# A reordered input stage in a one-core hybrid layer: one meta-token load, its Newton step on ScalarE, table products behind idle ones

## The chip, the cores and the metric

The kernel runs on one core of one Trainium2 chip. The metric is the device time of one launch in microseconds. A core has five engines with a queue of their own each: TensorE (PE, matmuls; PEld is its weight load), VectorE (DVE), ScalarE (ACT), GpSimd (POOL) and SyncE (SP, which here only issues DMAs). ACT issues DMAs too.

## The reference

One decoder layer with two token mixers, on 1024 tokens of width 1024 behind 16 meta tokens, all in float32:

```
h = concat([meta_tokens, x], axis=1)                  # 1040 rows
h = layer_norm(h, in_ln_g, in_ln_b)
z = h @ w_in + b_in                                   # -> q, k, v, conv input, gates
y_attn = sliding_window_attention(q, k, v, sinks, rel_bias) @ w_attn_proj
y_conv = silu(layer_norm(causal_dwconv(val * sigmoid(gate)))) @ w_conv_proj
mixed  = sigmoid(g_attn) * y_attn + sigmoid(g_conv) * y_conv
h = layer_norm(2**0.25 * h + mixed @ w_out, ln1_g, ln1_b)
f = (gelu(g) * u) @ ffn_w_down                        # u, g = causal_dwconv(h @ ffn_w_up)
out = layer_norm(2**0.25 * h + f, ln2_g, ln2_b)[:, 16:]
```

The attention bias depends on the distance of query and key alone, through a table of 32 buckets by 8 heads (`rel_bias`). The first layer norm, the scaled `h` of the first residual, and the rows of that bias table are what this document is about.

## The kernel before, in words

Every large product is done in three passes of a reduced float type: the operands are split into a high part (`hi`, `RHO`) and a rest (`lo`, `RHC`), and PE adds `hi*lo`, `hi*hi`, `lo*hi`. Each weight tile of 128 columns (512 KB) is loaded by SP into one of two raw buffers (`wr`), cast to its high part on ACT (L304) and subtracted to its rest on DVE (L307), and used for all 1040 rows.

The input stage (up to about 56 us) works on tiles of 128 tokens: the meta tokens as tile -1 (`xm`; two copies of the 16 rows, so that a transpose puts them where both neighbours need them) and x0 to x7. `tokens` groups them into (-1), (0, 1), (2, 3, 4), (5, 6, 7). For each group there are these steps, each a small function:

- `stat` (L431): statistics on DVE, two halves of 512 columns and one aggregate per tile;
- `table` (L461): on ACT the approximate inverse root of the variance, `r`;
- `newton` (L466): on DVE one Newton step on `r`, and `m = -mean * r`; four small instructions per group;
- `norm` (L475): `x * r + m`, in two halves, on DVE or ACT;
- `turns` (L492): PE transposes the tile in blocks `k` of 128 columns into PSUM; `scaled` (L505) applies the layer norm's g and b on ACT;
- `parts`, `high`, `low`: the split into `RHO` and `RHC`;
- `z_first` (L546): products of the first three weight tiles `first` (k, v and the first q tile). For the first group of rows, k and v are multiplied unsplit (`raw`).

The order of work on each engine here is written out by hand: `dv`, `ac` and `pe` chain the instructions of DVE, ACT and PE in the order of the text (L572 to L661), and `after` puts one instruction behind another on the same engine without a semaphore. Everything else is ordered by a planner, which takes a priority (`tc.cur_priority`, set by `rank`) and simulated times; loads of the input stage have hand-given ranks 5 to 25, and SP issues them in that order: meta twice (L197), x0, x1, the columns of small parameters (`coll`, `colr`), the second and the first weight tile, x2, the third weight tile, x3 to x7, the fourth weight tile when its buffer is free, the bias table (`tab`), and g and b of the layer norm (`gb`).

PE begins with 20 products of a constant with itself (`ps_w`, L575), whose results nobody uses. The rows of the bias by distance come from two products of `tab` (`ps_v`, L667), 400 and 164 columns wide, placed by the planner behind the input stage; DVE copies them to `vrow` (L668), SP stores `vrow` to `v1d`, spreads that over 128 rows in DRAM (`vd`), and loads from it the skewed `bias` tiles of attention.

`residual` (L288) forms `alpha * h` for the first residual from `x`, the mean, `r`, and the vectors `gb`, and stores it to `h0d`. On its first call it scales `gb` by alpha (L291), on DVE, behind the fourth weight tile's split (`last_split[3]`). All of it runs on DVE from about 50 to 75 us, while PE works on the next weight tiles. The convolution's 31 taps per channel block (L729) then fill DVE up to attention.

Of the kernel before, what the change touches and what calls it, by code (L numbers as in the profile page):

```python
# [38 lines left out]
NH = 8  # L39
# [9 lines left out]
ALPHA = 2.0 ** 0.25  # L49
# [30 lines left out]
J_BAND, J_META, J_META0, J_METAQ, J_LEN = 0, 384, 400, 544, 564  # L80
# [32 lines left out]
def tile_hybrid_layer(  # L113
# [3 lines left out]
    nc = tc.nc  # L117
# [5 lines left out]
    def load(o, i):  # L123
        return nc.sync.dma_start(out=o, in_=i)
# [57 lines left out]

    eps = const2.tile([P, 1], F, name="eps")
    nsink = const2.tile([P, 2 * NH], F, name="nsink")[:, :NH]
    with rank(0):
        nc.vector.memset(eps, EPS)
        nc.scalar.activation(nsink[:, 0:1], eps, AF.Abs_reciprocal_sqrt)

# [5 lines left out]
        nc.gpsimd.memset(xm[32:64], 0.0)  # L194
        nc.gpsimd.memset(xm[64:96], 0.0)
    with rank(5):
        for i in range(2):  # L197
            load(xm[i * NMETA:(i + 1) * NMETA], meta_tokens)
    xt = []

    def load_x(j):
# [15 lines left out]
    cff, ident = (coll[:, a - n_right:b - n_right] for a, b in COLS[2:-1])  # L217


    tab = sp.tile([P, J_LEN + NH], F, name="tab")  # L220
    with rank(0):
        nc.gpsimd.memset(tab, 0.0)
    with rank(25):
        load(tab[:33], table_in)

    def bcol(m):
        return colA[:, m:m + 1]
# [58 lines left out]
    gb_scaled = []  # L286

    def residual(src, mu, rs, n, first, dst):  # L288
        if not gb_scaled:
            gb_scaled.append(1)  # L290
            after(nc.vector.tensor_scalar(gb, gb, ALPHA, None, OP.mult), last_split[3])  # L291
        src = src[:n]
        nc.vector.scalar_tensor_tensor(src, src, mu[:n], gb[:n, 0], OP.subtract, OP.mult)
        nc.vector.scalar_tensor_tensor(src, src, rs[:n], gb[:n, 1], OP.mult, OP.add)
        load(dst, src[first:n])

# [134 lines left out]
    def stat(t, *js):  # L431

        J = len(tokens[t])
        if t not in norms:
            norms[t] = [sp.tile([P, J, 2], F, name=f"mv{t}")] + [sp.tile([P, J], F, name=f"{n}{t}") for n in "trm"]
        for j in js:
            x_, n = src_of(j)
            st_ = small.tile([P, 2, 6], F, name="st")
            for i in range(2):
                dv(V.bn_stats(st_[:n, i], x_[:, i * 512:(i + 1) * 512]))  # L440
            dv(V.bn_aggr(norms[t][0][:n, tokens[t].index(j)], st_[:n].rearrange("p a b -> p (a b)")))
# [19 lines left out]
    def table(t):  # L461
        mv, t_, r_, m_ = norms[t]
        n = src_of(tokens[t][0])[1]
        ac(nc.scalar.activation(r_[:n], mv[:n, :, 1], AF.Abs_reciprocal_sqrt, bias=eps[:n], scale=1.0))

    def newton(t):  # L466
        n = src_of(tokens[t][0])[1]
        mv, t_, r_, m_ = (x_[:n] for x_ in norms[t])
        stt = V.scalar_tensor_tensor
        dv(stt(t_, mv[:, :, 1], EPS, r_, OP.add, OP.mult))  # L470
        dv(stt(t_, t_, -0.5, r_, OP.mult, OP.mult))
        dv(stt(r_, t_, 1.5, r_, OP.add, OP.mult))
        dv(stt(m_, mv[:, :, 0], -1.0, r_, OP.mult, OP.mult))

    def norm(t, j, on_dve):  # L475
        x_, n = src_of(j)
        i = tokens[t].index(j)
        mv, t_, r_, m_ = norms[t]
        xns[j] = sp.tile([P, D], F, name="xn", tag="xn", bufs=4) if j >= 0 else xm
        to = xns[j] if j >= 0 else xm[96:]  # L480
        for a in range(0, D, 512):
            if on_dve:
                dv(V.tensor_scalar(to[:, a:a + 512], x_[:, a:a + 512], r_[:n, i:i + 1], m_[:n, i:i + 1], OP.mult, OP.add))
            else:
                ac(nc.scalar.activation(to[:, a:a + 512], x_[:, a:a + 512], AF.Identity, bias=m_[:n, i:i + 1],
                                        scale=r_[:n, i:i + 1]))
        later.append((x_, mv[:n, i, 0:1], r_[:n, i:i + 1], n, j))

    GT = [(-1, 0, 1), (2, 3, 4), (5, 6, 7)]
    turned, tms = {}, {}  # L490
# [42 lines left out]
    def whigh(i):  # L533
        ac(nc.scalar.copy(first[i][0], first[i][2]))
# [36 lines left out]

    tc.cur_priority = RK_START  # L572
    warm = pat.tile([P, 512], F, name="ps_w", tag="o")
    for i in range(20):
        pe(nc.tensor.matmul(warm[:, :P], ones, ones, start=True, stop=True))  # L575
# [12 lines left out]
    stat(2, 2)  # L588
    scaled(0, 0)
# [8 lines left out]
    evac(0, 0)  # L598
    stat(2, 3)
    stat(2, 4)  # L600
    whigh(1)
    table(2)
    z_first(0, (1,), *range(8), raw=True)
    evac(0, 1)
    newton(2)
# [54 lines left out]
        evac(2, i)  # L660
    first_nm = dv_done[-1]  # L661

    tc.cur_priority = RK_RESID + 1000
    vrow = sp.tile([P, J_LEN + 104], F, name="vrow")[:NH, :J_LEN]
    for a, b in ((0, 400), (400, J_LEN)):
        ps = pat.tile([P, 512], F, name="ps_v", tag="o" if a == 0 else "t", bufs=1 if a == 0 else 2)
        after(nc.tensor.matmul(ps[:NH, :b - a], tab[:, J_LEN:], tab[:, a:b], start=True, stop=True), pe_done[-1])  # L667
# [5 lines left out]
    tc.cur_priority = RK_RESID  # L673
    for src, mu, rs, n, j in later:
        if j >= 0:
            residual(src, mu, rs, n, 0, h0d[2 + j * P:2 + (j + 1) * P, :])
        else:
            residual(src, mu, rs, NMETA, U0, h0d[0:2, :])
    start.close()
# [1121 lines left out]
def packed(i):  # L1801

    def by_channel(*vs):
        return np.concatenate([np.reshape(v, (-1, P)) for v in vs]).T

    def heads(a):

        n = a.shape[1:]
        return a.reshape((NKV, NH // NKV, HD) + n).swapaxes(0, 1).reshape((CW,) + n)

    def tiles(w, c):

# [39 lines left out]
```

## Time and profile before

| | |
|---|---|
| median of 3 runs | 1262.14 us (1261.92 to 1262.55) |
| the profiled execution | 1261.79 us, span 1260.0 us |
| mean granted TensorE clock | 0.997 |
| PE busy | 1245.9 us (99%) |
| DVE, ACT busy | 1076.2 us (85%), 595.2 us (47%) |
| HBM read, written | 150.29 MB, 62.70 MB |

The span runs from the first to the last instruction of the profiled execution; its time as a launch is 1.8 us longer. Rows of the timeline give the start (us), the time taken (us), engine, line, operation, output and inputs, how many instructions of that form follow each other, and in brackets how long the engine was idle before and what ended that. Rows of the chain of waits give start, share in us, and engine, output and line. A row of the waits by engine gives engine, line, what it waited for, and the total, count and longest of these waits.

### The profile page before, as it was taken

The numbers are of one execution on the slowest core, as the hardware profiler recorded it, in microseconds if no ns is written. First come the engines' busy times: TensorE is split into PE (matmuls) and PEld (weight loads), VectorE is DVE, ScalarE is ACT, GpSimd is POOL, SyncE is SP. The second block draws the span as 40 slices with busy tenths as digits, with TensorE's granted clock in tenths as the row PEclk, the third lists the DMA queues.
The fourth block names the chain that finished last, engine by engine and source line by source line (L and its number), as shares of the span: only waits on it lengthen the run. The fifth ranks groups of instructions, "written<-read, shape, count | busy, mean of one in ns | idle before, by whom it ended". The sixth has DMA issues, their size and how long they took to land.

```text
span 1260.0 us, 23038 instructions
## 1 busy us (share of the span) xinstructions
PE 1245.9 (99%) x9186; PEld 1179.6 (94%) x9186; DVE 1076.2 (85%) x1858; ACT 595.2 (47%) x1100; POOL 7.9 (1%) x9
## 2 busy tenths in 40 slices
PE   8999999999999999999999999999999999999997
PEld 7999999999999999788899999999999998888886
DVE  7888999999978677448999999998989977996697
ACT  7532355655474233344655455455555544545330
POOL 0000000001000000000000000000000000000000
PEclk9999999999999999999999999999999999999999
DMA  6375633433256564221245545454454567998712
GB/s 255 104 253 148 183 108 97 106 93 85 72 155 172 167 166 118 84 99 70 67 161 204 188 171 214 160 209 139 159 205 160 196 227 251 394 357 320 271 63 84
DMA packets 98702, 212.19 MB, mean 168 GB/s; under 512 B 11412, under 2 KB 38612, under 8 KB 98339
## 3 DMA queue, kind: packets, MB, share of 16 engines
q1 hardware_dynamic: 84474, 199.64, 47.6%
q10 hardware_dynamic: 14120, 11.08, 2.8%
q8 instruction: 72, 1.18, 0.4%
q14 instruction: 36, 0.29, 0.1%
HBM read 150.29 MB, written 62.70 MB: 169 GB/s over the span
## 4 chain that ended last, share of the span: by engine, by line
PE 94%; DVE 3%; DMA 1%; ACT 1%; issue 1%; SPq 0%; DVEq 0%; ACTq 0%
PE px L1553 15%; PE py L1553 9%; PE ps_x L1698 9%; PE ps_z L342 8%; PE ps_z L345 8%; PE ps_z L346 8%; PE ps_p L1152 7%; PE ps_z L1698 5%; PE pz L1553 5%; PE pw L1553 5%; PE ps_w L342 2%; PE ps_w L345 2%; PE ps_w L346 2%; PE ps_z L560 2%; PE ps_t L923 1%; PE ps_h L503 1%
## 5 line engine op out<-in xcount | busy, mean ns | idle before, releaser
L342 PE MATMUL ps_z<-RHO,w 128*128 128x256 f32 (+2 forms) x864 | 243.4, 282 | 0.0
L345 PE MATMUL ps_z<-RHO,w 128*128 128x256 f32 (+2 forms) x864 | 242.3, 280 | 0.0
L346 PE MATMUL ps_z<-RHC,w 128*128 128x256 f32 (+2 forms) x864 | 242.2, 280 | 0.0
L342 PEld LDWEIGHTS ps_z<-RHO,w 128*128 128x128 f32 x864 | 162.5, 188 | 1.1 <-ACT FA L709 0.7
L345 PEld LDWEIGHTS ps_z<-RHO,w 128*128 128x128 f32 x864 | 162.5, 188 | 0.5
L346 PEld LDWEIGHTS ps_z<-RHC,w 128*128 128x128 f32 x864 | 162.7, 188 | 0.2
L729 DVE SCALAR_TENSOR_TENSOR FA<-cin,cdw,FA 128x1026 f32<-128x1026 f32 x120 | 154.3, 1296 | 0.7
L1375 DVE TENSOR_TENSOR RHO<-wr,RHO 128x512 fp32r<-128x512 f32 x94 | 63.6, 685 | 8.5 <-ACT RHO L1374 8.5
L304 ACT CAST w<-wr 128x1024 fp32r<-128x1024 f32 x37 | 38.8, 1048 | 61.9 <-PE ps_z L346 47.5
L1374 ACT CAST RHO<-wr 128x512 fp32r<-128x512 f32 x94 | 56.6, 619 | 22.7 <-DVE wr L1392 11.4
L1392 DVE TENSOR_TENSOR wr<-wr 128x512 f32<-128x512 f32 x88 | 60.2, 684 | 0.1
L738 ACT ACTIVATE FA<-ps_z,colr 128x258 f32<-128x258 f32 (+1 forms) x64 | 30.1, 472 | 60.5 <-PE ps_z L346 50.2
L307 DVE TENSOR_TENSOR w<-wr,w 128x1024 fp32r<-128x1024 f32 x37 | 45.1, 1218 | 9.5 <-ACT w L304 9.3
L1565 ACT COPY FA<-px 128x514 f32<-128x514 f32 (+2 forms) x23 | 13.2, 572 | 78.7 <-PE px L1553 78.7
L1152 PE MATMUL ps_p<-OC,w 128*128 128x256 f32 (+1 forms) x384 | 48.1, 278 | 0.0
L1152 PE MATMUL ps_p<-OA,w 128*128 128x256 f32 (+1 forms) x384 | 47.8, 278 | 0.0
L1152 PEld LDWEIGHTS ps_p<-OC,w 128*128 128x128 f32 x384 | 46.2, 188 | 0.1
L1152 PEld LDWEIGHTS ps_p<-OA,w 128*128 128x128 f32 x384 | 45.9, 188 | 0.0
L1375 DVE TENSOR_TENSOR w<-wr,w 128x512 fp32r<-128x512 f32 x60 | 40.6, 686 | 4.7 <-ACT w L1374 4.7
L1553 PE MATMUL px<-OA,RHO 128*128 128x258 f32 x324 | 43.2, 282 | 0.0
L1480 ACT ACTIVATE FA<-OB,coll 128x512 f32<-128x512 f32 x44 | 35.9, 816 | 14.7 <-DVE OB L1561 14.7
L1374 ACT CAST w<-wr 128x512 fp32r<-128x512 f32 x60 | 36.3, 618 | 12.3 <-DVE wr L1392 5.1
(443 smaller groups left out, 3088.1 us busy)
## 6 DMA issues: line engine op xcount, KB each, us to landing
wr<-in_w_up_dram SPq DMA_DIRECT2D x44, 512.0 KB, 3.6
wr<-in_w_z_dram SPq DMA_DIRECT2D x29, 512.0 KB, 4.0
OB<-in_w_down_dram SPq DMA_DIRECT2D x24, 512.0 KB, 4.9
fd<-FA SPq DMA_DIRECT2D x44, 256.0 KB, 2.0
FA<-sd SPq DMA_DIRECT2D x15, 512.0 KB, 8.7
qt<-qd SPq DMA_DIRECT2D x28, 256.0 KB, 5.0
OB<-td SPq DMA_DIRECT2D x14, 512.0 KB, 8.7
sgd<-FA ACTq DMA_DIRECT2D x48, 128.0 KB, 3.3
```

The costliest lines, as they stand in the source:

```text
L304: ins = nc.scalar.copy(hi, raw)
L307: return nc.vector.tensor_tensor(lo, raw, f32(hi), OP.subtract)
L342: ins = nc.tensor.matmul(ps, al, bh, start=i == 0, stop=False)
L345: nc.tensor.matmul(ps, ah, bh, start=False, stop=False)
L346: last = nc.tensor.matmul(ps, ah, bl, start=False, stop=i == n - 1)
L729: nc.vector.scalar_tensor_tensor(acc[c], cin[:, j:j + U], wc, acc[c], OP.mult, OP.add)
L1152: nc.tensor.matmul(ps[:, :b - a], x, rhs(k, hl, a, b), start=k + j == 0, stop=k == 3 and j == 2)
L1374: nc.scalar.copy(hi, src)
L1375: ins = nc.vector.tensor_tensor(lo, src, f32(hi), OP.subtract)
L1392: ins = nc.vector.tensor_tensor(*x)
L1553: ins = nc.tensor.matmul(o, x[:, ks], bmat(sub, q, hl, k), start=first and k + j == 0, stop=k == 3 and j == 2, skip_group_check=not first)
L1698: nc.tensor.matmul(banks[i], l[:, ts], r[:, ws], start=first and a and x + k == 0, stop=z and x == len(ops) - 1 and k == 2, skip_group_che ...
```

## The change

- `meta_tokens` is laid out twice on the host, and one load of 32 rows takes the place of two of 16.
- `tab` is cleared on DVE, not GpSimd, at the head of DVE's queue, and loaded through ACT's DMA queue ahead of ACT's first activation, not late on SP's.
- Idle products: 15, not 20. The two `ps_v` products follow directly behind them. Their PSUM copies: 164 columns on DVE behind `scales`, 400 columns on ACT at the end of its chain. `vrow` is stored from there at a higher rank.
- Meta's Newton step runs on ACT (`newton_act`, seven activations), so that `newton(0)` leaves DVE's chain. The normalization of `xm` stands in two halves on ACT, the second behind `table(1)`.
- `table(2)` stands ahead of the cast of the second weight tile (`whigh(1)`).
- Ranks of the first three weight loads: 13, 16, 19 in place of 14, 13, 16. The order of loads becomes x0, x1, columns, first weight tile, x2, second weight tile, x3, x4, third weight tile, x5 and so on.
- `gb` is scaled at the end of DVE's chain, ahead of the fourth weight tile's rest; the residual's first instruction on each tile except x0 is put behind that rest.

```diff
     with rank(0):
         nc.vector.memset(eps, EPS)
-        nc.scalar.activation(nsink[:, 0:1], eps, AF.Abs_reciprocal_sqrt)
+        nc.vector.memset(tab, 0.0)
+        tab_in = store(tab[:33], table_in)
+        after(nc.scalar.activation(nsink[:, 0:1], eps, AF.Abs_reciprocal_sqrt), tab_in)
...
-        for i in range(2):
-            load(xm[i * NMETA:(i + 1) * NMETA], meta_tokens)
+        load(xm[:2 * NMETA], meta_tokens)
...
-    tab = sp.tile([P, J_LEN + NH], F, name="tab")
-    with rank(0):
-        nc.gpsimd.memset(tab, 0.0)
-    with rank(25):
-        load(tab[:33], table_in)
...
-    def residual(src, mu, rs, n, first, dst):
-        if not gb_scaled:
-            gb_scaled.append(1)
-            after(nc.vector.tensor_scalar(gb, gb, ALPHA, None, OP.mult), last_split[3])
+    def residual(src, mu, rs, n, first, dst, behind=True):
         src = src[:n]
-        nc.vector.scalar_tensor_tensor(src, src, mu[:n], gb[:n, 0], OP.subtract, OP.mult)
+        ins = nc.vector.scalar_tensor_tensor(src, src, mu[:n], gb[:n, 0], OP.subtract, OP.mult)
+        if behind:
+            after(ins, last_split[3])
...
-        with rank({1: 14, 2: 13, 3: 16, 4: 23}.get(n, RK_SPLIT)):
+        with rank({1: 13, 2: 16, 3: 19, 4: 23}.get(n, RK_SPLIT)):
...
+            if n == 4:
+                after(last_split[-1], gb_scale)
...
+    c15 = sp.tile([P, 1], F, name="c15")
+    nc.vector.memset(c15, 1.5)
...
+    def newton_act(t):
+        n = src_of(tokens[t][0])[1]
+        mv, t_, r_, m_ = (x_[:n] for x_ in norms[t])
+        act = lambda *x, **y: ac(nc.scalar.activation(*x, AF.Identity, **y))
+        act(m_, mv[:, :, 0], scale=-1.0)
+        act(t_, mv[:, :, 1], bias=eps[:n], scale=1.0)
+        for i in range(2):
+            act(t_, t_, scale=r_)
+        act(t_, t_, bias=c15[:n], scale=-0.5)
+        act(t_, t_, scale=r_)
+        act(m_, m_, scale=t_)
+        norms[t][1:3] = norms[t][2:0:-1]
...
-    for i in range(20):
+    for i in range(15):
         pe(nc.tensor.matmul(warm[:, :P], ones, ones, start=True, stop=True))
+    ps_v = []
+    vrow = sp.tile([P, J_LEN + 104], F, name="vrow")[:NH, :J_LEN]
+    for a, b in ((0, 400), (400, J_LEN)):
+        ps = pat.tile([P, 512], F, name="ps_v", tag="o" if a == 0 else "mm", bufs=1 if a == 0 else 3)
+        pe(nc.tensor.matmul(ps[:NH, :b - a], tab[:, J_LEN:], tab[:, a:b], start=True, stop=True))
+        ps_v.append((a, b, ps))
     stat(0, -1)
     table(0)
+    newton_act(0)
+    norm(0, -1, False, (0,))
     stat(1, 0)
-    newton(0)
-    norm(0, -1, False)
     stat(1, 1)
     table(1)
+    norm(0, -1, False, (512,))
     newton(1)
     norm(1, 0, True)
     norm(1, 1, False)
     scales()
+    dv(V.tensor_copy(vrow[:, 400:], ps_v[1][2][:NH, :J_LEN - 400]))
...
+    table(2)
     whigh(1)
-    table(2)
...
-    tc.cur_priority = RK_RESID + 1000
-    vrow = sp.tile([P, J_LEN + 104], F, name="vrow")[:NH, :J_LEN]
-    for a, b in ((0, 400), (400, J_LEN)):
-        ps = pat.tile([P, 512], F, name="ps_v", tag="o" if a == 0 else "t", bufs=1 if a == 0 else 2)
-        after(nc.tensor.matmul(ps[:NH, :b - a], tab[:, J_LEN:], tab[:, a:b], start=True, stop=True), pe_done[-1])
-        after(nc.vector.tensor_copy(vrow[:, a:b], ps[:NH, :b - a]), first_nm)
+    ac(nc.scalar.copy(vrow[:, 0:400], ps_v[0][2][:NH, :400]))
+    gb_scale = dv(V.tensor_scalar(gb, gb, ALPHA, None, OP.mult))
+    tc.cur_priority = RK_QKV
     load(v1d, vrow)
...
-        "x": i["x"], "meta_tokens": i["meta_tokens"], "cols": cols,
+        "x": i["x"], "meta_tokens": np.concatenate([i["meta_tokens"]] * 2), "cols": cols,
```

More of the change, by code (lines that the diff above doesn't have):

```diff
@@ L184, in tile_hybrid_layer @@
     nsink = const2.tile([P, 2 * NH], F, name="nsink")[:, :NH]
+    tab = sp.tile([P, J_LEN + NH], F, name="tab")
     with rank(0):
         nc.vector.memset(eps, EPS)
-        nc.scalar.activation(nsink[:, 0:1], eps, AF.Abs_reciprocal_sqrt)
+        nc.vector.memset(tab, 0.0)
+        tab_in = store(tab[:33], table_in)
+        after(nc.scalar.activation(nsink[:, 0:1], eps, AF.Abs_reciprocal_sqrt), tab_in)
     xm = sp.tile([P, D], F, name="xm")
@@ L285, in tile_hybrid_layer @@
     load(gb[:, :, :].rearrange("p a b -> p (a b)"), dram(ln0_in, 0, [[0, P], [1, 2 * D]]))
-    gb_scaled = []
-    def residual(src, mu, rs, n, first, dst):
-        if not gb_scaled:
-            gb_scaled.append(1)
-            after(nc.vector.tensor_scalar(gb, gb, ALPHA, None, OP.mult), last_split[3])
+    def residual(src, mu, rs, n, first, dst, behind=True):
         src = src[:n]
-        nc.vector.scalar_tensor_tensor(src, src, mu[:n], gb[:n, 0], OP.subtract, OP.mult)
+        ins = nc.vector.scalar_tensor_tensor(src, src, mu[:n], gb[:n, 0], OP.subtract, OP.mult)
+        if behind:
+            after(ins, last_split[3])
         nc.vector.scalar_tensor_tensor(src, src, rs[:n], gb[:n, 1], OP.mult, OP.add)
@@ L473, in newton, with norm @@
         dv(stt(m_, mv[:, :, 0], -1.0, r_, OP.mult, OP.mult))
-    def norm(t, j, on_dve):
+    def newton_act(t):
[10 more added lines that the diff above has]
+        norms[t][1:3] = norms[t][2:0:-1]
+    def norm(t, j, on_dve, halves=(0, 512)):
         x_, n = src_of(j)
@@ L478, in norm @@
         mv, t_, r_, m_ = norms[t]
-        xns[j] = sp.tile([P, D], F, name="xn", tag="xn", bufs=4) if j >= 0 else xm
+        if halves[0] == 0:
+            xns[j] = sp.tile([P, D], F, name="xn", tag="xn", bufs=4) if j >= 0 else xm
         to = xns[j] if j >= 0 else xm[96:]
-        for a in range(0, D, 512):
+        for a in halves:
             if on_dve:
@@ L486, in norm @@
                                         scale=r_[:n, i:i + 1]))
-        later.append((x_, mv[:n, i, 0:1], r_[:n, i:i + 1], n, j))
+        if halves[-1]:
+            later.append((x_, mv[:n, i, 0:1], r_[:n, i:i + 1], n, j))
     GT = [(-1, 0, 1), (2, 3, 4), (5, 6, 7)]
@@ L675, in tile_hybrid_layer @@
         if j >= 0:
-            residual(src, mu, rs, n, 0, h0d[2 + j * P:2 + (j + 1) * P, :])
+            residual(src, mu, rs, n, 0, h0d[2 + j * P:2 + (j + 1) * P, :], j > 0)
         else:
```

## The prediction

> **What bounds the kernel now.** I read the page first, then what TensorE (PE) waited for, then the chain of waits over the first 25 us, then the timeline of each engine there.
>
> ```profile
> span 1260.0 us, 23038 instructions
> PE 1245.9 (99%) x9186; PEld 1179.6 (94%) x9186; DVE 1076.2 (85%) x1858; ACT 595.2 (47%) x1100; POOL 7.9 (1%) x9
> PE 94%; DVE 3%; DMA 1%; ACT 1%; issue 1%; SPq 0%; DVEq 0%; ACTq 0%
> ```
>
> PE is busy for 99% of the span and carries 94% of the chain that ended last. The other engines matter where they make PE wait. The view of waits, for PE from 30 us to the end of the matmuls, has three rows (engine and line, what it waited for, us in total, times, longest); the largest and the smallest:
>
> ```profile
> PE pw L1553 <- ACT FA L1355: 1.0, 1, 1.0
> ...
> PE ps_s L899 <- DVE sm L903: 0.3, 1, 0.3
> ```
>
> So PE waits hardly ever in over 1200 us. Each wait hangs on work that began after some PE result, so when PE starts earlier the wait moves with it. Hence two kinds of saving reach the end of the kernel one to one: an earlier start of the dense PE work, and matmuls taken out of the dense stretch. The chain of waits shows where the dense work starts:
>
> ```profile
> 1.64 3.58 DMA x<-in_x_dram
> 5.24 1.30 DVE st L440 x2
> ...
> 8.92 0.30 ACT r L464
> ...
> 13.01 1.27 PE ps_z L557 x2
> ...
> 14.71 0.46 PE ps_z L557 x2
> ```
>
> The first sequence tile lands, VectorE (DVE) takes statistics of it and of the second tile, ScalarE (ACT) takes the inverse root at 8.92, DVE normalizes, PE transposes, and its first products with weights start at 13.01. After 13.01 the chain is PE almost throughout. The timeline shows what else stands on these engines in that time:
>
> ```profile
> 0.74 0.86 SPq L124 DMA_DIRECT2D xm<-in_meta_tokens_dram  x2
> ...
> 0.86 0.17 DVE L241 MEMSET ones<- 128x128 f32 x1
> ...
> 1.08 6.16 PE L575 MATMUL ps_w<-ones 128*128 128x128 f32 x40 [1.08 <-DVE ones L241]
> ...
> 2.03 0.20 ACT L187 ACTIVATE nsink<-eps 128x1 f32<-128x1 f32 x1
> ...
> 3.64 1.27 DVE L440 BATCH_NORM_STATS2 st<-xm 32x6 f32<-32x512 f32 x2 [2.60 <-DMA xm<-in_meta_tokens_dram]
> ...
> 5.18 0.29 ACT L464 ACTIVATE r<-mv,eps 32x1 f32<-32x1 f32 x1 [2.95 <-DVE mv L441]
> ...
> 6.69 0.09 DVE L470 SCALAR_TENSOR_TENSOR t<-mv,r 32x1 f32<-32x1 f32 x1
> ...
> 7.27 1.27 DVE L440 BATCH_NORM_STATS2 st<-x 128x6 f32<-128x512 f32 x2
> 7.38 1.51 ACT L485 ACTIVATE xm<-xm,m,r 32x512 f32<-32x512 f32 x2 [1.90 <-DVE m L473]
> ...
> 8.29 0.30 PE L503 MATMUL ps_h<-coll,xm 128*128 128x128 f32 x1 [1.04 <-ACT xm L485]
> ...
> 10.63 0.33 PE L503 MATMUL ps_h<-coll,xn 128*128 128x128 f32 x1 [2.04 <-DVE xn L483]
> ```
>
> PE's 20 idle products fill it to 7.24; then it idles 1.04 and 2.04 us, and its first transposes of a sequence tile come at 10.63. Two stretches by engine (length, busy us of PE, its weight loads, DVE, ACT and GpSimd, granted clock, share of the DMA engines, GB/s):
>
> ```profile
> 7.53:10.94 3.41, 0.61 (x4) 0.45 (x5) 2.77 (x9) 2.57 (x5) 0.00 (x0) 1.00 1.00 402
> 10.94:14.36 3.42, 3.39 (x15) 2.65 (x13) 2.43 (x9) 2.59 (x5) 0.00 (x0) 0.50 1.03 418
> ```
>
> The transfers run at 402 GB/s, and the clock is 0.50 in the second stretch.
>
> **Part 1, the start of the chain.** One meta load instead of two takes one issue, 0.86/2 = 0.43 us, off SyncE's queue ahead of every x load. So x0's statistics, at 5.24 now, could start at about 4.8. Against that, the table's load, moved to ACT's queue at the head, runs beside x0: about 74 KB (33 x 572 floats) at 402 GB/s is 0.18 us. I take 4.9. From x0's statistics to those of x1 there are 7.27 - 5.24 = 2.03 us, of which 7.27 - 6.69 = 0.58 are meta's four Newton instructions. Without them x1's statistics start at 4.9 + 1.45 = 6.35. From there to the inverse root it is 8.92 - 7.27 = 1.65, so DVE is ready at 8.0. Is x1 there at 6.35? It did not wait at 7.27; 512 KB at 402 GB/s behind x0 is 1.3 us, so 6.2: barely.
>
> ACT must be free by then. Meta's statistics start 0.43 earlier, 3.2, and their inverse root 5.18 - 3.64 = 1.54 later, 4.74. Newton on ACT is seven instructions; the trace has no such chain. The nearest rows for one are 0.20 (L187) and 0.29 (L464, one operand taken per row). Most of the seven take such an operand, so I use 0.29 and 0.02 of gap: with the inverse root 8 x 0.31 = 2.5, to 7.2. Half of meta's normalization (1.51/2 = 0.76) ends at 8.0. Both engines arrive together, and the other half lies under DVE's Newton step of x0 and x1. I take 8.07 against 8.92: **0.85 us earlier**. Lower end: each instruction at 0.45 puts the inverse root at 4.74 + 0.29 + 7 x 0.45 + 0.76 = 8.94, no gain. Upper end: DVE's, 0.92 + 0.18.
>
> The Trainium skill ("ScalarE: Activation LUTs", Rules for kernel authors) says add and mul belong on VectorE, not ScalarE; that speaks against this move, and by its section on load costs (186 ns, plus 93 per row operand) the seven come to an estimated 2.0 us where DVE needed 0.58. By that price ACT would reach the second root at 7.7, DVE at 8.0 would be the later one, and the sum would be 0.07 us larger; the profile before doesn't show the chain on ACT.
>
> The table's memset moves from GpSimd to DVE's head: `ones` took 0.17 for 128 columns, so 572 cost at most 0.76; `ones` and the idle products begin that much later. Meta's statistics start only at 3.2, so DVE has room. ACT's own first instructions wait for this memset and the DMA issue (0.43), and end at 2.23 today, so at most 0.76 + 0.87 + 0.43 = 2.06 later, 4.3; the first inverse root comes at 4.74. Price if that cover fails: the difference, one to one.
>
> **Part 2, the products of the table.** Now they stand inside the dense stretch, behind one stationary group each:
>
> ```profile
> 64.17 0.28 PE L346 MATMUL ps_z<-RHC,w 128*128 128x256 f32 x1
> ...
> 64.50 0.28 PE L346 MATMUL ps_z<-RHC,w 128*128 128x256 f32 x1
> 64.71 0.84 PE L667 MATMUL ps_v<-tab 128*8 128x400 f32 x2
> ...
> 65.82 0.29 PE L346 MATMUL ps_z<-RHC,w 128*128 128x256 f32 x1
> ...
> 71.22 0.29 PE L346 MATMUL ps_z<-RHC,w 128*128 128x272 f32 x1
> 71.43 0.45 PE L667 MATMUL ps_v<-tab 128*8 128x164 f32 x2
> ...
> 72.15 0.28 PE L346 MATMUL ps_z<-RHC,w 128*128 128x256 f32 x1
> ```
>
> From one L346 to the next, three steps, it is 64.50 - 64.17 = 0.33 undisturbed. So the first pair costs 65.82 - 64.50 - 0.33 = 0.99, the second 72.15 - 71.22 - 0.33 = 0.60, less 0.03 for its wider neighbours (272 columns): **1.56 us**. They go behind 15 idle products. Five fewer of those free 5/20 x 6.16 = 1.5 us, the pair takes about 1.3, and the start is up to 0.76 later, so PE is done by 7.8 us, before anything waits for it at 9.8. The cover is PE's idle time; it fails only if the table lands after about 8.5.
>
> **Part 3, the scale vector and the copies.**
>
> ```profile
> 46.64 0.56 DVE L523 TENSOR_TENSOR RHC<-tm,RHO 128x384 fp32r<-128x384 f32 x1
> 49.11 1.23 DVE L307 TENSOR_TENSOR w<-wr,w 128x1024 fp32r<-128x1024 f32 x1 [1.91 <-ACT w L304]
> 50.25 1.22 DVE L291 TENSOR_SCALAR gb<-gb 128x2048 f32<-128x2048 f32 x1
> ```
>
> The scaling (1.22) fits into the 1.91 us pause ahead of 49.11. Nothing on PE waits for it directly. It, and the two table copies that leave DVE's later queue, start the residual and the convolution earlier. A further wait goes:
>
> ```profile
> DVE cin L717 <- DMA v1d<-vrow: 3.3, 1, 3.3
> ```
>
> because the table's row is written near 47, ahead of the residual and not behind it. All this is DVE time under a busy PE. It reaches PE only in its 0.3 us wait on DVE (L899); I count **0.3**, ends -0.5 (a new order on DVE) and 0.5. The other edits (load order with x2 ahead of the second weight tile, the inverse root of group 2 ahead of a weight cast) give DVE and ACT slack in the first 30 us, and nothing by themselves.
>
> **The sum.** 0.85 + 1.56 + 0.3 = 2.7 us. The profiled execution took 1261.79 (span 1260.0); the median of the runs is 1262.14, 0.35 above. So 1259.1 by the one, 1259.4 by the other; I say 1259.3.
>
> **Rivals.** *The clock stays full.* After a stretch with 0.61 us of PE work the clock was 0.50 for 3.42 us; a pair of products took 1.27 instead of 0.46. The forecast leaves that as it is. With transposes from 9.8 the same stretch would hold about 1.4 us of PE work, and if that suffices a further 0.7 us goes (one pair's 0.81, a little of it in ACT's time): 1258.6. For it: more than double the work. Against: the threshold isn't shown. The Trainium skill ("TensorE: Matmul & The Clock Gate", What's actually happening) has the clock halved after an idle window of 3.4 us, with windows that run freely; by that rule no window here is idle, and this rival is the outcome.
>
> *Newton on ACT is as slow as what it replaced*, or x1 lands late: part 1 gives nothing, 1.56 to 1.86 remain: 1260.4. It decides from 0.45 us an instruction.
>
> *A weight load falls behind the bias loads.* With the table's row ready before the residual, the order worked out for SyncE's queue can change.
>
> ```profile
> SPq L124 <- DMA vd<-v1d: 10.6, 1, 10.6
> 76.36 0.64 SPq L124 DMA_DIRECT2D wr<-in_w_z_dram  x1
> 91.48 1.05 ACT L304 CAST w<-wr 128x1024 fp32r<-128x1024 f32 x1 [1.69 <-PE ps_z L346]
> 93.61 4.41 SPq L124 DMA_DIRECT2D bias<-vd  x3
> 98.06 1.15 SPq L124 DMA_DIRECT2D biasq<-vd  x1
> wr<-in_w_z_dram SPq DMA_DIRECT2D x29, 512.0 KB, 4.0
> ```
>
> A weight load issued at 76.36 lands 4.0 later and is cast at 91.48, 11.1 us of slack. The block of bias loads with its wait holds the queue 10.6 + 4.41 + 1.15 = 16.2 us. Ahead of that load it costs 5.1, net 2.4 slower, and 1264.5; two loads hit cost more. It decides from 13.8 us of delay. Against it: the row is ready earlier, so the wait should shrink.
>
> **How the numbers follow.** Forecast 0.45, clock full 0.23, no gain at the start 0.21, the slow queue 0.11. A measurement here tells about 0.2%, 2.5 us, from no change, so the line is 1259.6. Two thirds of the forecast case and all of the full clock lie below it, 0.54; no gain at the start and the rest of the forecast lie within, 0.35; the slow queue is 0.11. The range leaves out the slow queue and little else. Low 1258.0: clock full, 1258.6, with part 1 at its upper end (0.25) and part 3 at its own (0.2), by the profile's base. High 1261.9: part 2 alone, 1260.6, with 0.5 lost on DVE and 0.8 at the start (Newton at 0.56 an instruction).
>
> **What would show it.** Right: the second inverse root near 8.1, first transposes near 9.8, seven ACT instructions of about 0.29, two ps_v pairs by 8 us, no gap at 64.7 and 71.4, gb scaled in a pause near 47. The clock in 10 to 15 us tells the first rival. Wrong: ACT reaching the second root after DVE, the table landing after 8.5, new PE waits after 80 us, or a weight cast that waits for its load.

## The result and the profile after

The kernel after takes 1258.65 us in the median (1258.11 to 1259.90), the kernel before beside it 1262.08 (1260.93 to 1262.55): a ratio of 0.9974, 95% interval 0.9965 to 0.9983. That is 3.4 us less, beyond the 0.2% that can be told from no change. The profiled execution took 1258.79, the one before 1261.79. First the page, with the same three lines as before:

```profile
span 1257.0 us, 23022 instructions
PE 1243.3 (99%) x9176; PEld 1178.3 (94%) x9176; DVE 1076.1 (86%) x1855; ACT 597.1 (48%) x1108; POOL 7.4 (1%) x8
PE 96%; DVE 2%; ACT 1%; DMA 0%; issue 0%; DVEq 0%; SPq 0%; ACTq 0%
```

PE is busy 2.6 us less and still for 99% of a shorter span. The chain of waits over the first 25 us says when each station was reached:

```profile
1.22 3.77 DMA x<-in_x_dram
...
5.01 1.30 DVE st L437 x2
...
8.08 0.30 ACT r L463
...
9.79 1.10 PE ps_h L517 x8
...
11.55 0.73 PE ps_z L571 x2
...
14.18 0.46 PE ps_z L571 x2
...
14.97 5.50 PE ps_z L571 x24
```

The second inverse root stands at 8.08 (8.92 before), the transposes at 9.79 (10.63), and a pair of products takes 0.73 and then 0.46, where before the first took 1.27. The timeline shows what makes the start shorter:

```profile
0.75 0.40 SPq L124 DMA_DIRECT2D xm<-in_meta_tokens_dram  x1
0.81 0.06 DVE L187 MEMSET eps<- 128x1 f32 x1 [0.81 <-PEq L1860]
0.96 0.54 DVE L188 MEMSET tab<- 128x572 f32 x1
...
3.15 1.27 DVE L437 BATCH_NORM_STATS2 st<-xm 32x6 f32<-32x512 f32 x2 [1.49 <-DMA xm<-in_meta_tokens_dram]
...
4.89 0.18 ACT L477 ACTIVATE m<-mv 32x1 f32<-32x1 f32 x1
4.98 0.28 ACT L477 ACTIVATE t<-mv,eps 32x1 f32<-32x1 f32 x1
...
6.51 1.29 DVE L437 BATCH_NORM_STATS2 st<-x 128x6 f32<-128x512 f32 x2
6.60 0.29 ACT L477 ACTIVATE m<-m,t 32x1 f32<-32x1 f32 x1
...
7.37 1.12 PE L594 MATMUL ps_v<-tab 128*8 128x400 f32 x4
```

Newton's seven instructions on ACT run from 4.89 to 6.89 (6.60 + 0.29) beside DVE's statistics, and the table's products fill a pause of PE. The granted clock in the two stretches that the prediction quoted (columns as there):

```profile
7.53:10.94 3.41, 2.37 (x16) 1.47 (x14) 2.87 (x13) 2.85 (x6) 0.00 (x0) 1.00 1.02 400
10.94:14.36 3.42, 3.08 (x20) 2.42 (x19) 3.32 (x9) 3.16 (x7) 0.00 (x0) 1.00 1.03 420
```

It stays at 1.00. I then took the matmuls of both traces in their order, without the idle and table products, and subtracted their starts: a **lead** of the kernel after, in us. It is 0.84 at the first transposes, 2.1 once the first transposes and pairs of products are through (15 to 30 us), 3.1 and 3.7 behind the places where the table's products stood (68 and 73 us). Then it shrinks: to 3.1 between 250 and 450 us, without any wait of PE, and to 2.1 across 605 us; 0.5 comes back by 620 and 0.4 near 1067, and 3.1 are left at the end. The loss at 605 has its row in PE's waits, and its place in the timeline:

```profile
PE pw L1572 <- ACT FA L1374: 1.2, 1, 1.2
PE px L1572 <- DVE OB L1327: 0.8, 1, 0.8
PE ps_s L918 <- DVE sm L922: 0.3, 1, 0.3
```

```profile
602.17 0.69 DVE L1327 TENSOR_TENSOR OB<-ps_w,OB 128x512 f32<-128x512 f32 x1 [1.44 <-PE ps_w L343]
...
602.92 1.63 PE L1572 MATMUL px<-OC,RHO 128*128 128x256 f32 x12 [0.78 <-DVE OB L1327]
```

The first product of the up-projection (`px`) waits until DVE has read the last `ps_w` of the stage before. In the kernel before it follows without a pause.

The 3.4 us hold two things. The time of the kernel before falls into two kinds by the mean granted clock of an execution. Of its 105 executions beside the experiments (one of 4421.79 us left out), 61 have a mean of 0.997 or less, median 1262.14 us, and 44 have 0.998 or more, median 1261.10. Of the 14 traces of this document, those with the lower mean are the five in which the clock was halved for 3.41 us after its first rise. Of the kernel after's eight executions, one has the lower mean (1259.90), and the other seven have a median of 1258.51. So with equal clock the change is worth 2.6 us, and the other 0.8 come from the halving being rarer.

### The profile page after: what moved, and what is told of

It is laid out like the page before. It is cut to its first block, busy times and chain, and to the rows that moved or that the text cites. A ratio compares the mean times of both kernels' runs of the same rounds, so it can differ in the third digit from the quotient of the medians.

```text
span 1257.0 us, 23022 instructions
## 1 busy us (share of the span) xinstructions
PE 1243.3 (99%) x9176; PEld 1178.3 (94%) x9176; DVE 1076.1 (86%) x1855; ACT 597.1 (48%) x1108; POOL 7.4 (1%) x8
## 4 chain that ended last, share of the span: by engine, by line
PE 96%; DVE 2%; ACT 1%; DMA 0%; issue 0%; DVEq 0%; SPq 0%; ACTq 0%
PE px L1572 15%; PE py L1572 10%; PE ps_x L1717 9%; PE ps_z L339 8%; PE ps_z L342 8%; PE ps_z L343 8%; PE ps_z L1717 7%; PE ps_p L1171 7%; PE pz L1572 5%; PE pw L1572 5%; PE ps_w L343 2%; PE ps_w L342 2%; PE ps_w L339 2%; PE ps_z L574 2%; PE ps_t L942 1%; PE ps_s L918 1%
## 5 line engine op out<-in xcount | busy, mean ns | idle before, releaser
L1572 PE MATMUL px<-OC,RHO 128*128 128x256 f32 x324 | 41.5, 277 | 0.8 <-DVE OB L1327 0.8
```

The source lines that it names most:

```text
L1572: ins = nc.tensor.matmul(o, x[:, ks], bmat(sub, q, hl, k), start=first and k + j == 0, stop=k == 3 and j == 2, skip_group_check=not first)
```

## Experiments

The theories at the outset. A: the steps of the prediction carry the gain, plus a clock that is not halved near 11 us, less 0.8 to 1.1 us lost at 602 us, because one `ps_v` tile now comes out of the three PSUM tiles of the ring `mm`, which turns the ring by one, so that `px` lands on the bank that is read last. B: in each case, that the step in question is worth nothing (or, where I had called it nothing, something). The versions ran in five groups, and the median of the kernel before beside them lay between 1261.33 and 1262.17 us; the intervals of most versions overlap with that of the kernel after, so a difference of a few tenths is weak by itself.

**The ring of PSUM tiles.** The idle products write two tiles of the ring in place of one of their own; with the `ps_v` tile that is a full turn.

```diff
-    warm = pat.tile([P, 512], F, name="ps_w", tag="o")
+    warms = [pat.tile([P, 512], F, name="ps_w", tag="mm", bufs=3) for _ in range(2)]
     for i in range(15):
+        warm = warms[i // 8]
```

> The changed kernel, with the idle products written into two PSUM tiles of the ring of three (mm) and not into the tile o. With the second table product that makes three tiles taken from that ring ahead of the first ps_z, so that every later tile falls on the bank it had in the kernel before. The order of all instructions is that of the changed kernel. Theory A: the changed kernel gave back about 1 us at 602 us, where px waited 0.78 for DVE's read of the last ps_w, because its one extra tile turned the ring by one and put the last ps_w on px's bank. Then the wait goes, px starts with the last ps_w product, and the median falls by 0.7 to 1.0, to about 1257.8. Theory B: DVE is simply later there for lack of time: the wait stays, 1258.6.

Measured: 1257.97 (1257.34 to 1259.56), ratio to before 0.9967 (0.9954 to 0.9979). In its timeline `px` no longer waits for DVE:

```profile
603.11 1.58 PE L1573 MATMUL px<-OC,RHO 128*128 128x256 f32 x12
```

The lead neither rises nor falls across 605 us (2.0 on both sides), and the time is 0.7 lower in the median, with intervals that overlap. By the trace theory A holds. This execution, the slowest of the six, also shows something else: its clock was halved, as before's was, from 11.62 us on.

```profile
8.21:11.62 3.41, 1.62 (x12) 1.39 (x13) 3.21 (x12) 3.19 (x6) 0.00 (x0) 1.00 1.02 411
11.62:15.03 3.41, 3.41 (x12) 2.60 (x12) 3.28 (x9) 2.01 (x5) 0.00 (x0) 0.50 1.04 422
```

By 16 us it had lost 1.5 us against the kernel after, with the same instructions. In the clock's own record this fall comes 6.83 us, twice 3.41, after the clock first rose (4.79 us), and so it does in the other four halved traces (4.12 and 10.95 in the kernel before). In the kernel after the clock rose at 5.93, so the stretch to set beside 8.21 to 11.62 is not one of the two quoted above but this:

```profile
9.34:12.76 3.42, 2.63 (x18) 2.23 (x19) 3.35 (x12) 3.25 (x6) 0.00 (x0) 1.00 1.03 419
```

Of the first experiment's 1.62 us of busy PE, 0.21 were products (from 11.41 on) and the rest transposes; of the kernel after's 2.63 us, 1.04 were products. The dense work begins at nearly the same time in both (11.41 and 11.55). What differs is where the stretches of 3.41 us fall.

**The clock in the kernel before.** 39 idle products in place of 20, nothing else:

```diff
-    for i in range(20):
+    for i in range(39):
```

> The kernel before with 39 idle products in place of 20 and nothing else; the order of all other instructions stays. Theory A: the halved clock from 10.9 to 14.4 us came from PE's idle stretch, 7.2 to 10.6, and cost about 1.2 us. Then with PE busy to about 11.3 the clock stays full; the transposes start 0.7 late, but dense work is 0.5 to 1.1 us ahead by 15 us: median about 1261.3. Theory B: the halving falls by chance of the window and not by PE's work: it is seen again or not, and the 0.7 us of delay remains: 1262.7.

Measured: 1263.41 (1262.66 to 1264.28), ratio 1.0012 (1.0003 to 1.0021). The clock was full from its first rise (6.60 us) on, but the idle products took longer than I had reckoned:

```profile
1.08 11.59 PE L575 MATMUL ps_w<-ones 128*128 128x128 f32 x78 [1.08 <-DVE ones L241]
```

They end at 12.67, the first transposes of a sequence tile came 2.0 us late, and by 66 us PE was only 0.9 late: some 1.1 us came back through the clock. So the clock is worth about what A says, and all eleven executions have a mean clock of 0.998 or more; but the time lies above what either theory gave: both took the added idle products to be shorter.

**Newton back on DVE.**

```diff
-    newton_act(0)
-    norm(0, -1, False, (0,))
     stat(1, 0)
+    newton(0)
+    norm(0, -1, False)
...
-    norm(0, -1, False, (512,))
```

> The changed kernel with meta's Newton step and its normalization back in the old place and order (four instructions on DVE between the statistics of x0 and x1). Theory A (the prediction's): these 0.58 us stand on the path to the second inverse root, which comes at 8.66 and not 8.08, and the end moves by the same 0.6: 1259.2. Theory B: x1's landing or ACT sets the second root, Newton's place is worth nothing: 1258.6.

Measured: 1259.19 (1258.88 to 1261.72), ratio 0.9982 (0.9973 to 0.9990), 0.54 slower than after; the second root comes at 8.61, not 8.08:

```profile
8.61 0.29 ACT L463 ACTIVATE r<-mv,eps 128x2 f32<-128x2 f32 x1
```

Theory A holds by the medians: 0.53 us at the first transposes are 0.54 us at the end. The two profiled executions end 0.29 apart, since that of the kernel after lost some lead between 250 and 450 us that this one kept.

**The table's products in their old place again**, into a tile that nobody reads, behind the same instructions as before:

```diff
+    tc.cur_priority = RK_RESID + 1000
+    again = pat.tile([P, 512], F, name="ps_a", tag="o", bufs=1)
+    for a, b in ((0, 400), (400, J_LEN)):
+        after(nc.tensor.matmul(again[:NH, :b - a], tab[:, J_LEN:], tab[:, a:b], start=True, stop=True), pe_done[-1])
```

> The changed kernel, with the two table products done a second time in the dense stretch, at their old place, into a PSUM tile that nobody reads. Order otherwise unchanged. Theory A (the prediction's part 2): PE is the bound there and the end moves by the whole price of the pair, 1.56 us: 1260.2. Theory B: later slack takes it up in part or in full: 1258.6 to 1259.5.

Measured: 1260.20 (1259.89 to 1261.91), ratio 0.9988 (0.9980 to 0.9997): 1.55 slower than after, and the 1.56 of the prediction. Theory A holds.

**Seven idle products in place of 15**, the rest as after (`range(7)`).

> The changed kernel with 7 idle products in place of 15; the order of everything else stays. PE is then done with the table's products near 6.5 us, and its next products other than transposes come at 11.5. Theory A: the clock is halved when a window of 3.41 us holds next to no such products, at whatever phase the windows fall; the gap of 5 us always holds one, so that the halving is seen in the trace and in nearly all executions: median 1259.9 to 1260.2 (1.2 to 1.5 more than the changed kernel), the front part of the gain gone again. Theory B: the clock doesn't depend on this gap: 1258.6.

Measured: 1260.84 (1259.54 to 1261.42), ratio 0.9989 (0.9981 to 0.9998): 2.2 slower. The chain of waits:

```profile
9.68 2.61 PE ps_h L517 x11
...
12.32 1.27 PE ps_z L571 x2
...
14.23 0.68 PE ps_z L571 x2
...
15.24 0.46 PE ps_z L571 x2
```

The transposes start earlier than in the kernel after (9.68), but the first pair of products takes the long 1.27, and PE is 1.9 us behind the kernel after by 16 us. The loss is larger than A's because the clock was not halved again: it had not risen at all before the dense work. Its record in this trace begins with a rise at 14.55 us (5.93 in the kernel after). The view of stretches gives 1.00 ahead of the first record, in this trace too, so there the length of the products has to be read.

**The ring, and three more idle products behind `ps_v`**, on the version of the first experiment:

```diff
+    for i in range(3):
+        pe(nc.tensor.matmul(warm[:, :P], ones, ones, start=True, stop=True))
```

> The changed kernel with the ring of PSUM tiles turned back as in the first experiment, and three more idle products behind the table's products, so that PE's gap ahead of its first real products is about 2.4 us and not 3.1. Theory A: no window fits the gap, the clock is never halved; every execution lies near 1257.6 and none above 1258.6. Theory B: halved executions come as often as before (in the first experiment the profiled one was, at 1259.56, of six): 1257.9, with one or two of ten above 1259.

Measured: 1257.78 (1257.48 to 1258.68), ratio 0.9967 (0.9955 to 0.9979); five of six executions lie within 1257.48 to 1257.89, the sixth above A's limit. No execution has the lower mean clock, as A has it; but in the first experiment it was one of six, so six without it don't tell A from B. PE's waits from 30 us on:

```profile
PE pw L1575 <- ACT FA L1377: 1.0, 1, 1.0
PE ps_s L921 <- DVE sm L925: 0.3, 1, 0.3
```

This is the fastest version: 0.9 below after in the median, though the two intervals overlap. Its lead over before is 3.6 from 73 us to 605 us, without loss, and 4.4 at the end.

**Two meta loads again.**

```diff
-        load(xm[:2 * NMETA], meta_tokens)
+        for i in range(2):
+            load(xm[i * NMETA:(i + 1) * NMETA], meta_tokens[:NMETA])
```

> The changed kernel with two loads of 16 meta rows in place of one of 32. Theory A (the prediction's): SyncE issues every x load 0.43 us later, and x0 stands first on the path: the second inverse root comes at 8.5, the end 0.4 later: 1259.05. Theory B: the transfers themselves, not their issue, set x0's landing: 1258.6.

Measured: 1258.92 (1258.40 to 1261.90), ratio 0.9982 (0.9973 to 0.9990): 0.27 slower, between the theories and nearer to A. The trace can't settle it, since x1 landed late in the profiled execution: its statistics start at 7.42, behind a wait for the load, and the second root comes at 8.99, not 8.5. This execution had the clock halved too:

```profile
9.29:12.70 3.41, 1.66 (x12) 1.42 (x13) 3.24 (x12) 3.20 (x5) 0.00 (x0) 1.00 1.02 416
12.70:16.11 3.41, 3.41 (x12) 2.60 (x12) 3.31 (x9) 2.04 (x5) 0.00 (x0) 0.50 1.02 416
```

**The old order of weight loads.**

```diff
-        with rank({1: 13, 2: 16, 3: 19, 4: 23}.get(n, RK_SPLIT)):
+        with rank({1: 14, 2: 13, 3: 16, 4: 23}.get(n, RK_SPLIT)):
```

> The changed kernel with the old ranks of the first three weight loads, so that x2 to x4 are loaded behind one more weight tile, 1.3 us later. Theory A (the prediction's): this order gives slack and nothing by itself: 1258.6 to 1258.9. Theory B: with PE 2.1 us ahead, group 2's statistics are late: its inverse root comes 1.3 later than 15.59, its rows are transposed late and part of the front gain is lost: 1259.4 to 1259.9.

Measured: 1259.88 (1259.38 to 1262.07), ratio 0.9986 (0.9977 to 0.9994), 1.2 slower. Here B holds: I had given this edit nothing by itself. The chain shows why:

```profile
17.61 0.29 ACT r L463
...
18.73 1.04 ACT w L548
19.77 1.42 ACT xn L498 x2
21.20 2.24 ACT RHO L532 x7
...
26.11 0.87 PE ps_h L517 x6
```

With x2 late, group 2's root comes at 17.61 (15.59 in the kernel after), and ACT's casts carry the chain where PE should; PE is 1.2 us later by 30 us, 0.4 of it from a later first transpose already.

**Part 3 undone.** The scale vector is formed again by the first residual call.

```diff
+    gb_scaled = []
...
+        if not gb_scaled:
+            gb_scaled.append(1)
+            after(nc.vector.tensor_scalar(gb, gb, ALPHA, None, OP.mult), last_split[3])
...
-            if n == 4:
-                after(last_split[-1], gb_scale)
...
-    gb_scale = dv(V.tensor_scalar(gb, gb, ALPHA, None, OP.mult))
```

> Part 3 undone: the residual's scale vector is formed again by the first residual call, behind the fourth split, and not in VectorE's pause; the rest is the kernel after. The planned order of later work moves with it on every engine, as it moved when part 3 was made. Theory A: part 3 is worth nothing, since the kernel after still had a PE wait of 0.3 at the sums (L918) and the first 600 us show no other PE wait on VectorE: 1258.65 within 0.4, and PE as far along at 400 us as in the kernel after, within 0.3. Theory B, the prediction's: 0.3 us are lost, about 1258.95, at one PE wait on VectorE. Theory C: the new order matters more than the 1.22 us of VectorE: the time lies over 0.5 from 1258.65, either way, and a row of PE's waits that the kernel after has not (or no longer) shows where.

Measured: 1261.53 (1260.18 to 1263.54), ratio to before 1.0002 (0.9992 to 1.0011): **all of the gain is gone**. In the trace the start is that of the kernel after. The lead falls from 3.7 to 3.1 across 74 us and from 3.1 to 1.6 across 151 us, and is 0.9 at the end. Besides, 0.3 us of the loss lie outside the span: a launch of this version takes 2.1 us more than its span in each execution, of the kernel after 1.8. PE's waits from 30 us on:

```profile
PE ps_s L920 <- DVE s L928: 1.3, 1, 1.3
...
PE px L1574 <- ACT OB L1586: 0.3, 1, 0.3
PE ps_z L342 <- DVE cin L738: 0.3, 1, 0.3
```

The first and the last are new against both kernels, and both are waits for DVE. DVE near 47 us, first here, then in the kernel after:

```profile
46.90 1.23 DVE L307 TENSOR_TENSOR w<-wr,w 128x1024 fp32r<-128x1024 f32 x1 [1.95 <-ACT w L304]
48.04 1.22 DVE L289 TENSOR_SCALAR gb<-gb 128x2048 f32<-128x2048 f32 x1
```

```profile
44.98 1.22 DVE L686 TENSOR_SCALAR gb<-gb 128x2048 f32<-128x2048 f32 x1
46.23 1.28 DVE L286 SCALAR_TENSOR_TENSOR x<-x,mv,gb 128x1024 f32<-128x1024 f32 x1
47.44 1.22 DVE L302 TENSOR_TENSOR w<-wr,w 128x1024 fp32r<-128x1024 f32 x1
```

With PE 3.7 us ahead of the kernel before, DVE is the engine that is late, unless its pause of 1.95 is filled. At 74 us the sum comes out: DVE's first copy of `cin` starts at 73.58, 2.92 earlier than in the kernel before (76.50), where DVE still had 0.20 to spare; PE is 3.71 earlier; 3.71 - 2.92 - 0.20 = 0.59, and 0.58 of lead are lost. At 151 us more has come between: from 74 to 152 us DVE waits 6.3 us for DMAs (2.6 for the taps `cdw`, 3.7 for stores of q's low part), in the kernel after 4.0 (1.3 and 2.7). Theories A and B fall; C's size fits. So the order of later work counts too, and the next three runs are about that.

**Part 3 alone, in the kernel before**: the same edit as in the change, there.

> Part 3 alone, put into the kernel before: the scale vector is formed in VectorE's pause near 47 us and the first residual step goes ahead of the split; the start and the table products are as before, and TensorE's order is that of the kernel before, instruction by instruction. With part 3 undone in the kernel after (the run before this one) 2.9 us were lost, at two PE waits on VectorE (0.3 near 74 us, 1.3 near 151 us) and in a new order of later work. Theory A: those waits arise only because PE is 3.6 us ahead there; in the kernel before, PE is late enough for VectorE to be ready, its only wait on VectorE at the sums is 0.3, so part 3 alone gives 0 to 0.4: 1261.7 to 1262.1 on the kernel before's own time of 1262.1. Theory B: the parts add up, part 3 is worth some 2.9 wherever it stands: about 1259.2. Theory C: the loss of the run before lay in its order of later work and not in VectorE's time; then part 3 alone, with the old order kept, gives nothing at all, and no PE wait in this trace differs by over 0.2 from that of the kernel before, the 0.3 at the sums (L899) included; A and C differ in that wait alone.

Measured: 1261.46 (1260.67 to 1262.42), ratio 0.9999 (0.9990 to 1.0008). Its wait at the sums is the old one:

```profile
PE ps_s L900 <- DVE sm L904: 0.3, 1, 0.3
```

Part 3 alone is worth nothing, the rest without it (in an order of its own) nothing, all together 3.4 us. B falls; A and C can't be told apart by this run.

**The scale vector on ACT, in the order of the run that undid part 3.**

```diff
-            after(nc.vector.tensor_scalar(gb, gb, ALPHA, None, OP.mult), last_split[3])
+            after(nc.scalar.activation(gb, gb, AF.Identity, scale=ALPHA), last_split[3])
```

> The kernel of the run that undid part 3, with one instruction moved: the scale vector is still formed behind the fourth split, but by ScalarE and not by VectorE; the order of all other instructions on PE, VectorE and SyncE is that of that run, one by one. VectorE so has 1.2 us less to do between 48 and 73 us. Theory A (VectorE's time decides): its residual steps and all behind them come up to 1.2 us earlier, the PE waits of 0.3 near 74 us and of 1.3 near 151 us shrink or go, and most of the 2.9 us come back: 1259.0 to 1260.0. Theory C (the order of later work decides): the order is the same, so the time stays: 1261.2 to 1261.8.

Measured: 1260.64 (1260.01 to 1263.68), ratio 0.9994 (0.9985 to 1.0003), between the two theories, 0.9 faster than with the scaling on DVE, some 0.15 of it outside the span. The waits on DVE shrink:

```profile
PE ps_s L920 <- DVE s L928: 0.5, 1, 0.5
PE ps_z L342 <- DVE cin L738: 0.2, 1, 0.2
```

In the trace the lead lost at 74 and 151 us is 1.24 in place of 2.10, so 0.86 come back. But DVE didn't get the 1.2 us that the edit was to free: it now waits for ACT to scale.

```profile
52.12 1.27 DVE L291 SCALAR_TENSOR_TENSOR xm<-xm,mv,gb 16x1024 f32<-16x1024 f32 x1 [1.06 <-ACT gb L289]
```

All of this execution runs 2.93 us later than the run before it (split at 49.83 for 46.90). Against that, DVE's residual block comes 0.11 earlier, and the loss at 74 us falls by 0.12 (0.46 for 0.58). The other 0.74 come back at 151 us, where three of DVE's waits for stores of q's low part are shorter, by 0.8 in all (3.53 to 3.07, and 0.13 and 0.18 to nothing). The longest of them, first with the scaling on DVE, then here:

```profile
122.41 0.43 DVE L398 TENSOR_TENSOR qsl<-FA,qsh 128x258 fp32r<-128x258 f32 x1 [3.53 <-DMA qd<-qsl]
```

```profile
124.95 0.43 DVE L398 TENSOR_TENSOR qsl<-FA,qsh 128x258 fp32r<-128x258 f32 x1 [3.07 <-DMA qd<-qsl]
```

So this run doesn't show what 1.2 us of DVE are worth. In this pair of traces the loss at 151 us goes with those waits, in an unchanged order.

**The first residual step behind the split, in the kernel after**: a part of the pause stays unused, PE's order is that of the kernel after.

```diff
-            residual(src, mu, rs, n, 0, h0d[2 + j * P:2 + (j + 1) * P, :], j > 0)
+            residual(src, mu, rs, n, 0, h0d[2 + j * P:2 + (j + 1) * P, :], True)
```

> The kernel after, in which the first residual step of the first tile stands behind the fourth split like the others, and not ahead of it in VectorE's pause; the scale vector keeps its place in the pause, and PE's order is that of the kernel after, one by one. Of the pause 0.7 us stay unused, so VectorE is about 0.7 us later at 72 us than in the kernel after. Theory A (VectorE's time decides): its slack there, 72.9 in the first pass of the convolution's copies against PE at 73.9, covers little; 0.2 to 1.0 us are lost, 1258.9 to 1259.7, with a PE wait on VectorE near 74 or 150 us. Theory C (the order of later work decides): PE's order is kept, so nothing is lost: 1258.65 within 0.25.

Measured: 1258.89 (1258.35 to 1259.96), ratio 0.9976 (0.9967 to 0.9986), 0.24 slower than after, at the edge of both expectations. No PE wait on DVE appears at 74 or 150 us: 0.7 us of lateness are still covered there. One of 0.4 at 515 us, on DVE's read of a `ps_w`, is not in the kernel after. So of the 2.9 us that undoing part 3 lost, the 0.6 at 74 us are shown to be DVE's lateness out of the residual block, the 1.5 at 151 us a wait for DVE that goes with its longer waits for DMAs, and 0.3 lie outside the span. Why these DMA waits are longer in that order I have not shown.

## Why the prediction was right or wrong

- **The start, 0.85: right.** 0.84 in the trace, each station of DVE within 0.16 of its number (x1's statistics 6.51 for 6.35 is the farthest). ACT was done 0.3 earlier than said (7.73 for 8.0) and waited 0.34 for DVE, so DVE alone set the second root. The runs split it by medians: Newton on ACT 0.54, the single meta load 0.27. That one pair of traces gives 0.84 is in part luck: x0 lands at a different time in each execution, and the second root came at 8.92, 9.37 and 9.63 in the three traces with the old input stage, at 7.94 to 8.21 in seven with the new one unchanged and at 9.25 in an eighth. Seven instructions cost 2.0 us (4.89 to 6.89) where DVE needed 0.58. The price in the Trainium skill ("ScalarE: Activation LUTs", What ACT_TABLE_LOAD costs), 186 ns and 93 more for a row operand in six of the seven, gives an estimated 1.9, close to that; its advice to keep add and mul off ScalarE (same page, Rules for kernel authors) did not decide here, since ACT was idle and DVE was not.
- **The table's products, 1.56: right**, 1.54 in the lead and 1.55 in the run that put them back. Two details were off: `ps_v` ended at 8.49 and not by 7.8. Five idle products fewer freed 0.54 us (6.16 - 5.62), not 1.5; and even that hangs on the execution, since the same 15 took 5.07 us in the first experiment and 6.15 in the one with three more behind them. The cover to 9.79 hid both.
- **The clock: wrong.** The forecast left it halved; the rival "clock stays full" is what the profile shows. The lead grows by 1.27 us where the rival had 0.7 for one pair of products: 0.62 of it in the transposes ahead of the first pair, which ran at half clock before and which the rival left out, 0.51 in the pair and 0.14 in the transposes behind it. The rival's reason was wrong too: it asked whether about 1.4 us of PE work would do, and stretches with 1.62 and 1.66 us were followed by half clock in two runs. The kernel after holds 2.63 us in its stretch because that begins later; whether the clock is halved changes from execution to execution, and the change only made it rarer.
- **Part 3, 0.3: wrong in kind.** I sized it by the one PE wait on DVE in the profile before, 0.3. That wait is still there. The step's worth is conditional: nothing where PE is late, and where PE is 3.7 us ahead 2.9 us by the medians (1261.53 - 1258.65), 2.4 by the profiled executions (1261.22 - 1258.79), the changed order of later work included. "When PE starts earlier the wait moves with it" was the sentence that failed. DVE's residual block near 50 to 73 us keeps its length, and its slack against PE was below what parts 1 and 2 brought.
- **"The other edits ... nothing by themselves": wrong** for the order of weight loads, which is worth 1.2 in the kernel after. Neither it nor the earlier inverse root of group 2 was tried in the kernel before, and the latter in no run.
- **Not foreseen: the ring of PSUM tiles**, 1.0 us of lead at 605 us, 0.7 by the medians. The prediction moved a product and did not ask which tiles its new place takes, and whose turn that shifts 600 us later.
- **The slow SyncE queue: did not happen.** Its wait for the row of the table fell from 10.6 to 5.7 us, as argued.

So in the profiled pair the number came out near by errors that cancel: 3.65 us of lead by 73 us instead of 2.7, since the clock stayed full, less what was given back later. With equal clock, as the forecast assumed, the medians are 2.6 apart against its 2.7, although the ring took 0.7 that it did not foresee; where that came back I can't say. The loss of 0.6 of lead between 250 and 450 us in the profiled execution has no wait beside it and is absent in the fastest version; it stays open.

## What to carry to other kernels

Before adding up savings of the bound engine, ask of the next engine how much slack it has at each later meeting point: a step that fills its pause can be worth nothing alone, and yet the whole gain can go when it is taken out, here in part through the order that changed with it. When an experiment is to free an engine, see in its trace whether the engine then waits for something else. When an operation moves, list the buffers of the rings that it now takes, since a ring turned by one can cost a wait far away. Near a throttle one trace is one draw: set executions of equal granted clock side by side before pricing a step.

## What the runs showed of the hardware

PE's clock was halved for 3.41 us in five of the 14 traces, each time 6.83 us after it had first risen. The 3.41 us ahead of each fall held 0.62 to 1.66 us of busy PE, of which 0 to 0.24 were products and the rest transposes. The first two stretches of that length behind the rise, where the clock was kept, held at least 2.25 us in every trace, at least 1.02 of it products. The Trainium skill ("TensorE: Matmul & The Clock Gate", What's actually happening) halves it after an idle window, which these were not by their busy time. The same page (Part 4: PE-mode transpose) says that a transpose "doesn't count as PE-busy the same way", and the runs agree with that; they don't show it, since the busy time alone parts the two groups as well. With seven idle products the clock first rose at 14.55 us and the first pair took 1.27 us, with 15 it rose at 5.93 and the pair took 0.73: a start with too little work on PE costs more at its first products than the idle ones do. And 1.22 us of work on one engine, placed in its pause or behind it, moved the whole by 2.4 to 2.9 us, the order of what follows having moved with it.
